# A conformer block on one core: order of the first projections, block sums of the up projection on VectorE, and a third plain pair

## The chip, the cores and the metric

The kernel runs on one core of a Trainium2 chip. The metric is the device time of one execution in microseconds; the time before is the median of three executions, 1815.06 us (1814.44 to 1816.28).

## What is computed

One layer of a hybrid block over 1024 tokens of width 1024, all in float32, cut here to what matters:

```python
h = rms_norm(x, norm1_g)
z = h @ w_in                                   # GLU value and gate, q, k, v, gate logits
a = a_val * sigmoid(a_gate)                    # the GLU: the "first projections"
a = silu(rms_norm(causal_depthwise_conv(a)))   # 31 taps
y_a = a @ w_conv_out
y_b = mixed_dilated_attention(q, k, v) @ w_attn_out
x = x + (g_a * y_a + g_b * y_b) @ w_out
h = rms_norm(x, norm2_g)
u = causal_depthwise_conv(h @ w_up)            # 1024 -> 2 x 2816, 3 taps
x = x + (silu(u_gate) * u_val) @ w_down
```

## The kernel before, in words

**Numbers and engines.** Every large product is made of matmuls on rounded operands: `split()` (L76, L77) copies a float32 tile to a rounded high part on ACT and subtracts it on DVE to get the low part, and each product is then three matmuls (high x high, high x low, low x high). So every operand, weights and activations, costs an ACT and a DVE operation before PE can use it. `stage()` (L81) loads a 128x1024 piece of weights into one of four `raw` buffers, `wsplit()` (L84 on) splits it into one of four `whi` and `wlo` buffers, `wpiece()` does both. PSUM is two double banks (`big_ps`, pool psA) and four single banks (`bank_ps`, pool psB).

**Who sets the order.** The code is written stage by stage, but a scheduler places each engine's instructions and may put an instruction ahead of others that stand earlier in the code, as far as buffers and data allow. An engine then works its list strictly in that order. So the order of the program text and the order on the engines differ.

**First stage (L204 to L240).** Eight token tiles of `x` are loaded; each is normalised (L221 to L223: squares on ACT, a power on POOL, a scaled multiply on DVE that writes `xs`), transposed on PE into two psum banks of psB (`tp_<tile>_<half of the channels>`, L190), and split from there into `hT` (L76, L77). `hT00` and `hT10` are the high and the low part of the first 512 tokens, `hT01` and `hT11` those of the other 512. The GLU loop (L227 on) then multiplies: `gemm_ch` runs `gemm_half` (L108 to L110) for the first 512 tokens (24 matmuls) and for the second (24), into a double bank per channel piece: `glug_0` (gate), `gluv_0` (value), and so on.

**The up projection (L541 to L658).** Its input (`h2raw`, transposed by `tq_<tile>_<half>`, L515, and copied by ACT, L516) and the weights are taken as 2x2 blocks, and the product is made with seven block products instead of eight, per pair `f` of a value and a gate channel piece (22 pairs). The activations' side needs the blocks b11, b12, b21, b22 and the sums t1 = b12 - b11, t3 = b22 - b12, t2 = t3 + b11 and t4 = b21 - t2, each split into `blk_t1` and so on. `sums(q)` does them for one half `q` of the columns at a time: t1 on POOL (L599), t3 and t2 on DVE (L600, L602); t4 follows on POOL (L619). The weights' side needs sums too (`up_sums`: L571 to L576 on DVE; `s12`, `s3g` and, split later, `s4`). The code of a pair: `up_first(f)` loads `raw_uv<f>` and makes the first two products (24 matmuls each pair of halves together, X and Z, of `h2left` with `hi_uv<f>`, `lo_uv<f>`) into the two halves of a double bank `xz_<f>`; these need no sums and are the "plain" products; `up_rest(f)` adds the products with t2, t1, t3, b22 and t4 (into X and a bank `y_<f>`), copies out on ACT (L631, L636, L643) and DVE (L632, L638, L641), applies the three taps and the gate (L647 to L652), and stores `dff[f]` (L653). Ahead of `sums(cols[1])` the code has the plain products of pairs 0 and 1.

**The down projection (L662 on)** loads `dff` (L676) and `w_down` (L682) in groups of two, again as seven block products into `dx_0`, `dx_1` (double banks) and four `dy` banks (`mac`, L703). The first two groups' activations are loaded ahead into `early0` and `early1`; the next go through tiles `gr` and, like the residuals `res` (L711), through memory that the blocks of the up projection hold until its last matmul. All DMAs named here are issued from SP's queue, in order.

## Time and profile before

| | |
|---|---|
| median of three executions | 1815.06 us (1814.44 to 1816.28) |
| the profiled execution | 1811.43 us |
| its span, from first to last instruction | 1809.6 us, so 1.8 us lie around it |
| granted TensorE clock, mean | 0.991 |

One execution was recorded. The profiled one is 3.6 us shorter than the median, so a time that is worked out from its rows is a difference, to be put on the median. A row of a timeline gives start, duration, engine, line, operation, output and inputs by the program's names without numbers, how many in a row, and in brackets the idle time before it with what ended it. A row of the waits gives the total in us, how often, and the longest. A row of the windows gives each engine's busy us, then the granted clock, the share of the DMA engines and GB/s. Engines are PE (TensorE), PEld (its weight loads), DVE (VectorE), ACT (ScalarE), POOL (GpSimd) and SP (SyncE). Matmuls overlap: one of 128x512 lasts 0.39 us and the next starts 0.23 us after it.

### The profile page before, as it was taken

The numbers are of one execution on the slowest core, as the hardware profiler recorded it, in microseconds if no ns is written. First come the engines' busy times: TensorE is split into PE (matmuls) and PEld (weight loads), VectorE is DVE, ScalarE is ACT, GpSimd is POOL, SyncE is SP. The second block draws the span as 40 slices with busy tenths as digits, with TensorE's granted clock in tenths as the row PEclk, the third lists the DMA queues.
The fourth block names the chain that finished last, engine by engine and source line by source line (L and its number), as shares of the span: only waits on it lengthen the run. The fifth ranks groups of instructions, "written<-read, shape, count | busy, mean of one in ns | idle before, by whom it ended". The sixth has DMA issues, their size and how long they took to land.

```text
span 1809.6 us, 22474 instructions
## 1 busy us (share of the span) xinstructions
PE 1765.8 (98%) x8244; PEld 1461.9 (81%) x8244; DVE 1318.8 (73%) x1798; ACT 771.6 (43%) x1202; POOL 195.8 (11%) x197
## 2 busy tenths in 40 slices
PE   7999999999999999999999999989999999999999
PEld 5888888888887888887888878768888888878887
DVE  5999999999735655666654543787777777789863
ACT  4111132232245656666655332545444554543441
POOL 1000133133002122222210000210000000000000
PEclk9999999999999999999999999999999999999999
DMA  5111145345549456666527543313222222389851
GB/s 203 59 47 47 41 134 163 116 134 157 157 173 246 145 158 175 180 165 179 164 70 279 169 160 133 104 48 107 80 82 81 71 95 91 116 303 335 298 180 47
DMA packets 142063, 257.57 MB, mean 142 GB/s; under 512 B 11265, under 2 KB 60545, under 8 KB 141953
## 3 DMA queue, kind: packets, MB, share of 16 engines
q1 hardware_dynamic: 141808, 255.61, 43.8%
q8 instruction: 65, 1.06, 0.3%
q10 hardware_dynamic: 144, 0.52, 0.1%
q14 instruction: 46, 0.37, 0.1%
HBM read 190.03 MB, written 66.06 MB: 142 GB/s over the span
## 4 chain that ended last, share of the span: by engine, by line
PE 53%; DMA 4%; DVE 4%; issue 1%; ACT 1%; SPq 1%; POOLq 0%; POOL 0%; DVEq 0%; ACTq 0%
PE xz L550 5%; PE xz L551 5%; PE xz L552 5%; PE dx L703 5%; PE dy L703 5%; DMA gg<-dya 2%; PE pp L400 2%; PE y L550 2%; PE y L552 2%; PE y L551 2%; PE ya L108 2%; PE ya L109 2%; PE ya L110 2%; PE o L408 2%; PE wo L126 1%; PE wo L127 1%
## 5 line engine op out<-in xcount | busy, mean ns | idle before, releaser
L253 DVE SCALAR_TENSOR_TENSOR cacc<-apad,pk,cacc 128x1024 f32<-128x1024 f32 x240 | 297.7, 1274 | 0.7
L125 PE MATMUL qkv<-hi_qkv,hT 128*128 128x512 f32 x384 | 151.8, 396 | 0.0
L127 PE MATMUL qkv<-hi_qkv,hT 128*128 128x512 f32 x384 | 150.0, 391 | 0.0
L126 PE MATMUL qkv<-lo_qkv,hT 128*128 128x512 f32 x384 | 149.4, 390 | 0.0
L389 DVE CUSTOM_DVE_ANT_0 p<-s,m 128x128 f32<-128x128 f32 (+7 forms) x128 | 95.1, 750 | 62.7 <-PE pp L400 39.0
L77 DVE TENSOR_TENSOR pl<-pp,ph 128x512 fp32r<-128x512 f32 x192 | 103.1, 549 | 49.1 <-ACT ph L76 48.6
L393 POOL TENSOR_SCALAR p<-p,st 128x128 f32<-128x128 f32 (+7 forms) x128 | 94.9, 748 | 335.5 <-DVE st L392 211.9
L76 ACT ACTIVATE ph<-pp 128x512 fp32r<-128x512 f32 x192 | 91.3, 487 | 92.2 <-PE pp L400 89.3
L649 DVE SCALAR_TENSOR_TENSOR u<-u,pk 128x1023 f32<-128x1023 f32 (+1 forms) x88 | 112.3, 1279 | 18.9 <-ACT u L647 18.5
L101 POOL TENSOR_TENSOR rs<-ss,mhalf 128x8 f32<-128x8 f32 (+1 forms) x40 | 80.3, 2010 | 353.1 <-DVE ss L100 353.0
L391 ACT ACTIVATE p<-p,st 128x128 f32<-128x128 f32 (+7 forms) x128 | 99.0, 776 | 14.6 <-DVE st L389 12.9
L108 PE MATMUL gate<-hT,hi_gt 128*128 128x512 f32 x256 | 101.8, 398 | 0.0
L109 PE MATMUL gate<-hT,hi_gt 128*128 128x512 f32 x256 | 100.8, 394 | 0.0
L110 PE MATMUL gate<-hT,lo_gt 128*128 128x512 f32 x256 | 100.3, 393 | 0.0
L400 PE MATMUL pp<-ident,p 128*128 128x128 f32 x576 | 94.4, 277 | 0.0
L127 PEld LDWEIGHTS qkv<-hi_qkv,hT 128*128 128x128 f32 x384 | 72.0, 188 | 15.3
L126 PEld LDWEIGHTS qkv<-lo_qkv,hT 128*128 128x128 f32 x384 | 72.2, 188 | 14.5 <-DVE lo_qkv L77 0.3
L125 PEld LDWEIGHTS qkv<-hi_qkv,hT 128*128 128x128 f32 x384 | 72.2, 188 | 14.0
L400 PEld LDWEIGHTS pp<-ident,p 128*128 128x128 f32 x576 | 69.5, 142 | 10.0 <-issue 0.2
L384 PE MATMUL s<-kh,q 128*128 128x512 f32 (+1 forms) x192 | 69.7, 368 | 7.3 <-DVE st L389 4.8
L408 PE MATMUL o<-ph,v 128*128 128x512 f32 x192 | 73.1, 381 | 3.6 <-ACT ph L76 1.8
L409 PE MATMUL o<-pl,v 128*128 128x512 f32 x192 | 70.5, 369 | 1.6 <-DVE pl L77 1.5
(269 smaller groups left out, 4610.4 us busy)
## 6 DMA issues: line engine op xcount, KB each, us to landing
wr<-w_down SPq DMA_DIRECT2D x45, 512.0 KB, 5.7
gr<-dff SPq DMA_DIRECT2D x62, 256.0 KB, 5.2
raw_qkv<-w_qkv SPq DMA_DIRECT2D x24, 512.0 KB, 3.9
raw_uv<-w_up SPq DMA_DIRECT2D x22, 512.0 KB, 3.3
raw_ug<-w_up SPq DMA_DIRECT2D x22, 512.0 KB, 3.3
dff<-u SPq DMA_DIRECT2D x22, 512.0 KB, 2.6
dv<-v SPq DMA_DIRECT2D x16, 512.0 KB, 3.2
raw_gt<-w_ch SPq DMA_DIRECT2D x16, 512.0 KB, 4.8
```

The lines of the kernel that those rows point to most:

```text
L108: pe.matmul(o, hi[:, k, :], ah[:, k, :], start=(k == 0), stop=False)
L109: pe.matmul(o, hi[:, k, :], al[:, k, :], start=False, stop=False)
L110: pe.matmul(o, lo[:, k, :], ah[:, k, :], start=False, stop=(k == KT - 1))
L125: pe.matmul(ps, ah, hi[:, k % 2, :], start=(k == 0), stop=False)
L126: pe.matmul(ps, ah, lo[:, k % 2, :], start=False, stop=False)
L127: pe.matmul(ps, al, hi[:, k % 2, :], start=False, stop=(k == KT - 1))
L253: dve.scalar_tensor_tensor(out=acc, in0=a[:, j : j + T], scalar=w(j), in1=acc, op0=ALU.mult, op1=ALU.add)
L400: pe.transpose(pp[:, qb * P : (qb + 1) * P], pts[qb][:, kt * P : (kt + 1) * P], ident)
L550: pe.matmul(o, wh[:, k, :], bh[:, k, :], start=(start and k == 0), stop=False, skip_group_check=not start)
L551: pe.matmul(o, wh[:, k, :], bl[:, k, :], start=False, stop=False, skip_group_check=not start)
L552: pe.matmul(o, wl[:, k, :], bh[:, k, :], start=False, stop=(k == 3), skip_group_check=not start)
L703: pe.matmul(banks[n], a[:, c], b[:, d], start=(start and i == 0 and m == 0), stop=(stop and i == nf - 1 and m == 2), skip_group_check=True)
```

## The change

Three edits. First, the code of the first stage normalises four tiles, splits the two first weight pieces, makes the first-half products of `glug_0` and `gluv_0`, then the other four tiles and the second halves; the two pieces' loads stay where they were. Second, `sums(q)` runs wholly on DVE: t13 = b12 - b11 (t1), t2 = b22 - t13 directly, then t13 is used again for t3 = b22 - b12; t4 moves from POOL to DVE. Third, the plain products of pair 2 are written ahead of the splits of b22 and t4; they go to two single banks `xzx_2` and `xzz_2` instead of a double bank.

```diff
+        def first_pair(half):
+
+            for ps, w in zip(glu0, wfirst):
+                for _ in gemm_half(ps[:, half * 512 : half * 512 + 512], w, hT, half):
+                    pass
+
+        for tt in range(4):
+            normed(tt)
+        wfirst = [wpiece(w_ch[c], n, raw) for c, n, raw in wfirst]
+        glu0 = [big_ps("glug_0"), big_ps("gluv_0")]
+        first_pair(0)
+        for tt in range(4, 8):
+            normed(tt)
+        first_pair(1)
...
-        def up_first(f):
+        def up_first(f, apart=False):
...
-            xz = big_ps(f"xz_{f}")
-            product(xz[:, 0:512], four(vh)[:, 0:4], four(vl)[:, 0:4], *left[0], True)
-            product(xz[:, 512:1024], four(vh)[:, 4:8], four(vl)[:, 4:8], *left[1], True)
+            if apart:
+                xz = (bank_ps(f"xzx_{f}"), bank_ps(f"xzz_{f}"))
+            else:
+                xz = big_ps(f"xz_{f}")
+                xz = (xz[:, 0:512], xz[:, 512:1024])
+            product(xz[0], four(vh)[:, 0:4], four(vl)[:, 0:4], *left[0], True)
+            product(xz[1], four(vh)[:, 4:8], four(vl)[:, 4:8], *left[1], True)
...
-            pool.tensor_tensor(out=t1, in0=b12[:, :, q], in1=b11[:, :, q], op=ALU.subtract)
-            dve.tensor_tensor(out=t3, in0=b22[:, :, q], in1=b12[:, :, q], op=ALU.subtract)
-            keep("t3", t3, q)
-            dve.tensor_tensor(out=t3, in0=t3, in1=b11[:, :, q], op=ALU.add)
-            keep("t2", t3, q)
-            keep("t1", t1, q)
-            t2.append(t3)
+            less = lambda o, x, y: dve.tensor_tensor(out=o, in0=x, in1=y, op=ALU.subtract)
...
+            less(t13, b12[:, :, q], b11[:, :, q])
+            less(t, b22[:, :, q], t13)
+            keep("t2", t, q)
+            keep("t1", t13, q)
+            less(t13, b22[:, :, q], b12[:, :, q])
+            keep("t3", t13, q)
+            t2.append(t)
...
         ups = [up_first(1)]
         sums(cols[1])
+        ups.append(up_first(2, True))
...
-            pool.tensor_tensor(out=t2[i], in0=b21[:, :, q], in1=t2[i], op=ALU.subtract)
+            dve.tensor_tensor(out=t2[i], in0=b21[:, :, q], in1=t2[i], op=ALU.subtract)
```

What the scheduler makes of it is seen in the order of instructions on the engines. The places below are in program order; a line number after the change is the one of the changed file, so L107 to L109 are the projections' matmuls, L189 the transposes, L532 `tq`, L567 to L569 the block products, L618 and L642 the sums, L726 `mac`, L699 the loads of `gr`, L734 the residuals.

**First place: PE in the first stage,** around the transposes of the last token tiles. Before, the transposes of tiles 4 and 5 stand 18 rows further up, among the first-half matmuls, and those of tiles 6 and 7 here:

```order
L109 MATMUL gluv_0_414<-hT10_190,hi_v0_168 128x512
L110 MATMUL gluv_0_414<-hT00_189,lo_v0_169 128x512
L190 MATMUL tp_6_0_326<-ident_70,xs_6_319 128x128 x4
L190 MATMUL tp_6_1_333<-ident_70,xs_6_319 128x128 x4
L190 MATMUL tp_7_0_347<-ident_70,xs_7_340 128x128 x4
L190 MATMUL tp_7_1_354<-ident_70,xs_7_340 128x128 x4
L108 MATMUL gluv_0_414<-hT00_189,hi_v0_168 128x512
L109 MATMUL gluv_0_414<-hT10_190,hi_v0_168 128x512
L110 MATMUL gluv_0_414<-hT00_189,lo_v0_169 128x512
L108 MATMUL glug_0_363<-hT01_191,hi_g0_162 128x512
L108 MATMUL gluv_0_414<-hT01_191,hi_v0_168 128x512
```

After, at the same rows:

```order
L108 MATMUL gluv_0_278<-hT10_182,hi_v0_273 128x512
L109 MATMUL gluv_0_278<-hT00_181,lo_v0_274 128x512
L189 MATMUL tp_4_0_334<-ident_70,xs_4_327 128x128 x4
L189 MATMUL tp_4_1_341<-ident_70,xs_4_327 128x128 x4
L189 MATMUL tp_5_0_355<-ident_70,xs_5_348 128x128 x4
L189 MATMUL tp_5_1_362<-ident_70,xs_5_348 128x128 x4
L189 MATMUL tp_6_0_376<-ident_70,xs_6_369 128x128 x4
L189 MATMUL tp_6_1_383<-ident_70,xs_6_369 128x128 x4
L189 MATMUL tp_7_0_397<-ident_70,xs_7_390 128x128 x4
L189 MATMUL tp_7_1_404<-ident_70,xs_7_390 128x128 x4
L107 MATMUL glug_0_277<-hT01_183,hi_g0_269 128x512
L107 MATMUL gluv_0_278<-hT01_183,hi_v0_273 128x512
```

All 48 first-half matmuls now stand ahead of the transposes of tiles 4 to 7, which follow one another; then comes the second half. The lists of ACT and DVE for this stage hold the same operations in the same order as before.

**Second place: PE and DVE where the up projection starts.** PE before, from the second-to-last transposes on; the other 21 matmuls of `xz_1` follow, and then twelve of `y_0` with `blk_t1`:

```order
L515 MATMUL tq_6_1_10120<-ident_70,x2_1_6_9987 128x128 x4
L550 MATMUL xz_1_10183<-h2left0_9424,hi_uv1_10179 128x512
L551 MATMUL xz_1_10183<-h2left0_9424,hi_uv1_10179 128x512
L515 MATMUL tq_7_0_10159<-ident_70,x2_1_7_10035 128x128 x4
L515 MATMUL tq_7_1_10165<-ident_70,x2_1_7_10035 128x128 x4
L552 MATMUL xz_1_10183<-h2left0_9424,lo_uv1_10180 128x512
L550 MATMUL xz_1_10183<-h2left0_9424,hi_uv1_10179 128x512
```

PE after; here `xz_1` is complete before `tq_7`, and four matmuls of the third pair stand ahead of `y_0`:

```order
L568 MATMUL xz_1_10183<-h2left1_9425,hi_uv1_10179 128x512
L569 MATMUL xz_1_10183<-h2left1_9425,lo_uv1_10180 128x512
L532 MATMUL tq_7_0_10159<-ident_70,x2_1_7_10035 128x128 x4
L532 MATMUL tq_7_1_10165<-ident_70,x2_1_7_10035 128x128 x4
L567 MATMUL xzx_2_10225<-h2left0_9424,hi_uv2_10221 128x512
L568 MATMUL xzx_2_10225<-h2left0_9424,hi_uv2_10221 128x512
L567 MATMUL xzz_2_10226<-h2left1_9425,hi_uv2_10221 128x512
L568 MATMUL xzz_2_10226<-h2left1_9425,hi_uv2_10221 128x512
L567 MATMUL y_0_10263<-blk_t1_10146,hi_s12_0_10131 128x512
L568 MATMUL y_0_10263<-blk_t1_10146,hi_s12_0_10131 128x512
L569 MATMUL y_0_10263<-blk_t1_10146,lo_s12_0_10132 128x512
```

The other 20 matmuls of the third pair follow behind the twelve of `y_0` with `blk_t1`, and then `y_0` with `blk_b22`. DVE before, from the first t3 difference on (POOL's t1 difference runs beside it):

```order
L600 TENSOR_TENSOR cb_t3_0_10149<-h2raw1_9423 128x1024
L538 TENSOR_TENSOR s1_7_10066<-ss2_9426 128x1
L100 TENSOR_SCALAR s1_7_10066<-s1_7_10066 128x1
L77 TENSOR_TENSOR blk_t1_10146<-cb_t1_0_10148,blk_t1_10146 128x4x256
L540 SCALAR_TENSOR_TENSOR x2_1_7_10035<-x2_1_7_10035,s1_7_10066,gb2_8796 128x1024
L77 TENSOR_TENSOR lo_uv1_10180<-raw_uv1_10177,hi_uv1_10179 128x1024
L77 TENSOR_TENSOR blk_t3_10147<-cb_t3_0_10149,blk_t3_10147 128x4x256
L77 TENSOR_TENSOR lo_s4_0_10274<-raw_uv0_10083,hi_s4_0_10273 128x512
L600 TENSOR_TENSOR cb_t3_256_10209<-h2raw1_9423 128x1024
L602 TENSOR_TENSOR cb_t3_0_10149<-cb_t3_0_10149,h2raw0_9422 128x1024
L77 TENSOR_TENSOR blk_b22_10175<-h2raw1_9423,blk_b22_10175 128x4x256 x2
L571 TENSOR_TENSOR s12_1_10314<-raw_ug1_10312 128x512
```

DVE after, from the first block sum on (`cb_t13` serves t1 and then t3):

```order
L618 TENSOR_TENSOR cb_t13_0_10148<-h2raw1_9423,h2raw0_9422 128x1024
L555 TENSOR_TENSOR s1_7_10066<-ss2_9426 128x1
L618 TENSOR_TENSOR cb_t2_0_10149<-h2raw1_9423,cb_t13_0_10148 128x1024
L99 TENSOR_SCALAR s1_7_10066<-s1_7_10066 128x1
L77 TENSOR_TENSOR lo_uv1_10180<-raw_uv1_10177,hi_uv1_10179 128x1024
L77 TENSOR_TENSOR blk_t1_10146<-cb_t13_0_10148,blk_t1_10146 128x4x256
L557 SCALAR_TENSOR_TENSOR x2_1_7_10035<-x2_1_7_10035,s1_7_10066,gb2_8796 128x1024
L77 TENSOR_TENSOR blk_t2_10145<-cb_t2_0_10149,blk_t2_10145 128x4x256
L618 TENSOR_TENSOR cb_t13_0_10148<-h2raw1_9423 128x1024
L642 TENSOR_TENSOR cb_t2_0_10149<-h2raw0_9422,cb_t2_0_10149 128x1024
L77 TENSOR_TENSOR blk_t3_10147<-cb_t13_0_10148,blk_t3_10147 128x4x256
L618 TENSOR_TENSOR cb_t13_256_10208<-h2raw1_9423,h2raw0_9422 128x1024
```

The subtraction of `blk_t3` for the first columns moves ahead of `blk_b22`; t4 of the first columns (L642) now stands here too; the second columns' `blk_t1` comes five rows behind the last one shown. On SP the load `raw_uv2` now comes ahead of `raw_ug1`, and its buffer is the one that `cb_t13_0` holds until `blk_t3` of the first columns is split.

**Third place: PE and SP at the end of the up projection.** PE before, the last matmuls of pair 21 and the first of the down projection; 47 more matmuls of `dx_0` and `dx_1` with `early0` and `early1` follow without a product of the up projection among them:

```order
L552 MATMUL xz_21_12867<-blk_t4_10176,lo_s3g_21_12903 128x512
L550 MATMUL xz_21_12867<-blk_t4_10176,hi_s3g_21_12902 128x512
L551 MATMUL xz_21_12867<-blk_t4_10176,hi_s3g_21_12902 128x512
L552 MATMUL xz_21_12867<-blk_t4_10176,lo_s3g_21_12903 128x512
L703 MATMUL dx_0_12997<-hi_a11_0_13009,early0_12992 128x512
L703 MATMUL dx_0_12997<-lo_a11_0_13010,early0_12992 128x512
```

PE after, where the last product of pair 21 (with `blk_t4`) begins:

```order
L726 MATMUL dx_0_12998<-hi_a11_2_13052,early1_12994 128x512 x2
L726 MATMUL dx_0_12998<-lo_a11_2_13053,early1_12994 128x512
L726 MATMUL dx_0_12998<-hi_a11_2_13052,early1_12994 128x512
L567 MATMUL xz_21_12868<-blk_t4_10176,hi_s3g_21_12903 128x512
L568 MATMUL xz_21_12868<-blk_t4_10176,hi_s3g_21_12903 128x512
```

And where that product of twelve matmuls ends:

```order
L567 MATMUL xz_21_12868<-blk_t4_10176,hi_s3g_21_12903 128x512
L568 MATMUL xz_21_12868<-blk_t4_10176,hi_s3g_21_12903 128x512
L569 MATMUL xz_21_12868<-blk_t4_10176,lo_s3g_21_12904 128x512
L726 MATMUL dx_1_12999<-hi_a11_0_13010,early0_12993 128x512
L726 MATMUL dx_1_12999<-lo_a11_0_13011,early0_12993 128x512
```

The 24 matmuls of `dx_0` with the early groups now stand ahead of that product, and the 24 of `dx_1` behind it. SP before:

```order
L682 DMA wr00_0_13224<-w_down 128x2x512
L711 DMA res_0_0_0_13041<-dx2_0_132 128x512
L711 DMA res_0_1_0_13043<-dx2_1_133 128x512
L711 DMA res_0_2_0_13045<-dx2_2_134 128x512
L711 DMA res_0_3_0_13047<-dx2_3_135 128x512
L676 DMA gr00_4_13079<-dff4_114 128x512
L676 DMA gr00_4_13079<-dff5_115 128x512
```

SP after:

```order
L705 DMA wr00_0_13225<-w_down 128x2x512
L676 DMA dff20_130<-u_20_12779 128x1024
L734 DMA res_0_0_0_13042<-dx2_0_132 128x512
L734 DMA res_0_1_0_13044<-dx2_1_133 128x512
L734 DMA res_0_2_0_13046<-dx2_2_134 128x512
L734 DMA res_0_3_0_13048<-dx2_3_135 128x512
L699 DMA gr00_4_13080<-dff4_114 128x512
L699 DMA gr00_4_13080<-dff5_115 128x512
```

The store of `dff20` now stands ahead of the residual loads; before it stood behind the `gr` loads.

25 lines of the change are left out of this document (13 added, 12 removed).

## Prediction

> **What bounds the kernel now.** The page comes first: which engine is full, and where it is not.
>
> ```profile
> span 1809.6 us, 22474 instructions
> ...
> PE 1765.8 (98%) x8244; PEld 1461.9 (81%) x8244; DVE 1318.8 (73%) x1798; ACT 771.6 (43%) x1202; POOL 195.8 (11%) x197
> ```
>
> TensorE is busy for 98% of the span. So the change is worth only what it takes from, or adds to, the 2% in which PE waits or runs at a lower clock. The waits of PE, read for the two stages that the change names (the first 60 us, then 1160 to 1210) and for the stage behind them, from 1610 on, are few:
>
> ```profile
> PE tp L190 <- DVE ss L100: 10.7, 2, 9.4
> PE glug L108 <- ACT hT L76: 0.5, 1, 0.5
> ...
> PE y L551 <- DVE blk_t L77: 4.7, 1, 4.7
> PE y L550 <- ACT hi_s L76: 2.7, 1, 2.7
> PE tq L515 <- issue: 0.8, 1, 0.8
> PE xz L550 <- ACT hi_uv L76: 0.8, 1, 0.8
> ...
> PE dx L703 <- ACT gh_t L76: 1.3, 1, 1.3
> ```
>
> Between 1210 and 1610 no wait is listed at all. The same in windows (busy time of PE, PEld, DVE, ACT and POOL, then the granted clock):
>
> ```profile
> 1160.00:1170.00 10.00, 8.39 (x44) 6.51 (x43) 9.62 (x10) 6.27 (x12) 3.03 (x3) 1.00 0.39 131
> 1170.00:1180.00 10.00, 5.30 (x24) 4.05 (x22) 10.00 (x9) 6.02 (x7) 3.00 (x1) 0.88 0.01 2
> 1180.00:1190.00 10.00, 9.73 (x33) 7.48 (x34) 10.00 (x10) 4.84 (x5) 3.30 (x1) 0.78 0.21 66
> 1190.00:1200.00 10.00, 7.33 (x33) 5.61 (x32) 8.47 (x9) 3.15 (x5) 3.30 (x1) 1.00 0.16 55
> ...
> 1210.00:1260.00 50.00, 49.89 (x218) 40.29 (x217) 41.09 (x45) 24.28 (x30) 0.00 (x0) 1.00 0.22 76
> ```
>
> In the 40 us where the up projection starts, PE is idle for 9.2 us (40 less 8.39, 5.30, 9.73 and 7.33) while DVE is full. Behind 1210 PE is full, DVE has 9 us of 50 free, and there is nothing to win. The lower clock of 1170 to 1190 is seen in the matmuls:
>
> ```profile
> 1174.79 0.39 PE L550 MATMUL y<-blk_t,hi_s 128*128 128x512 f32 x1
> 1179.88 0.80 PE L551 MATMUL y<-blk_t,hi_s 128*128 128x512 f32 x1 [4.70 <-DVE blk_t L77]
> ...
> 1180.90 0.63 PE L550 MATMUL y<-blk_t,hi_s 128*128 128x512 f32 x1
> ...
> 1184.31 0.42 PE L552 MATMUL y<-blk_t,lo_s 128*128 128x512 f32 x1
> ...
> 1196.15 0.50 PE L550 MATMUL y<-blk_b,hi_s 128*128 128x512 f32 x1 [2.67 <-ACT hi_s L76]
> ```
>
> After the idle 4.70 us eight matmuls take 3.41 us (1180.90 to 1184.31), 0.426 each; later the pitch is 0.227 (48 of them from 1594.47 to 1605.35, quoted below). So ten slow matmuls cost another 2.2 us, and everything that this stage can give is 9.2 + 2.2 = 11.4 us. After the 2.67 us wait, no such stretch follows.
>
> **The first stage.** The scheduler of the kernel before already starts the projections on half of the tokens, as the timelines of PE, ACT and DVE show:
>
> ```profile
> 20.18 0.80 PE L108 MATMUL glug<-hT,hi_g 128*128 128x512 f32 x1 [0.48 <-ACT hT L76]
> ...
> 27.60 1.91 PE L190 MATMUL tp<-ident,xs 128*128 128x128 f32 x16
> ...
> 34.15 1.91 PE L190 MATMUL tp<-ident,xs 128*128 128x128 f32 x16
> ...
> 37.35 0.50 PE L109 MATMUL glug<-hT,hi_g 128*128 128x512 f32 x1
> ...
> 34.78 2.07 ACT L76 ACTIVATE hT<-tp 128x512 fp32r<-128x512 f32 x4 [4.48 <-PE tp L190]
> ...
> 35.41 2.48 DVE L77 TENSOR_TENSOR hT<-tp,hT 128x512 fp32r<-128x512 f32 x4 [3.33 <-ACT hT L76]
> ```
>
> The order of ACT and DVE here does not change; PE's does. Before, the transposes of tiles 4 and 5 (27.60) lie among the first half's matmuls, and their splitting on ACT and DVE is hidden by those. After, all 48 first-half matmuls run first: 45 of them and 16 transposes (27.60 to 29.27, when the matmuls resume: 1.67) were done at 34.15, so without those transposes 48 are done at 34.15 - 1.67 + 3 x 0.227 = 33.2. Then come 32 transposes into four psum banks, so tile 6 waits for DVE to empty the banks of tile 4. DVE's first subtraction starts 1.26 us after the transposes begin (34.15 to 35.41), at 34.4, and one takes 0.60 ((2.48 - 0.68)/3). The second half's first matmul with the rounded remainder of hT (37.35 before) needs seven of them: 34.4 + 7 x 0.605 = 38.7. **+1.4 us**, and PE is full behind it, so all of it stays. Bounds: 0, if the order made nothing late, and +2.2, if all eight are needed and a bank's turn adds 0.2.
>
> **The start of the up projection.** The four 128x1024 operations of POOL go (L599, L619), and DVE gets four more. The rows give one of POOL's, then DVE's scaled multiply beside it and alone, and two whole splittings that follow on each other:
>
> ```profile
> 1160.19 2.43 POOL L599 TENSOR_TENSOR cb_t<-h2raw,h2raw 128x1024 f32<-128x1024 f32 x1 [0.55 <-ACT h2raw L516]
> ...
> 1160.29 3.41 DVE L540 SCALAR_TENSOR_TENSOR x<-x,s,gb 128x1024 f32<-128x1024 f32 x1
> ...
> 1167.18 1.28 DVE L540 SCALAR_TENSOR_TENSOR x<-x,s,gb 128x1024 f32<-128x1024 f32 x1
> 1168.38 1.22 DVE L77 TENSOR_TENSOR lo_uv<-raw_uv,hi_uv 128x1024 fp32r<-128x1024 f32 x1
> 1169.51 1.22 DVE L77 TENSOR_TENSOR blk_t<-cb_t,blk_t 128x1024 fp32r<-128x1024 f32 x1
> ```
>
> One operation beside each POOL operation is stretched by about 2.1 us (3.41 against 1.28). Ahead of blk_t1, for which PE waits at 1179.88, lie two such stretches, 4.3 us. In their place stand five more whole operations (three differences and two splittings, 1.13 us each by the pitch 1168.38 to 1169.51, 5.7 in all) and two half ones fewer (1.2): DVE wins nothing by then.
>
> Step by step: PE begins uv0 at 1159.7, and runs 48 uv matmuls (10.9) and two pairs of tq (0.8 each) without the waits of 0.8 us, since ACT rounds uv1 ahead of the block sums: free at 1172.1. Next in its order stand four matmuls of the third pair, which wait for hi_uv2, and **behind them queue y_0's twelve and all else on PE**. The load of uv2 is issued when DVE has split t3 of the first columns and so emptied a raw buffer: fifteen DVE operations from 1158.0 on (ten whole ones of 1.13, two scaled of 1.19, 0.8 in short ones, none stretched) end at 1172.7. Then 3.3 us for the load (the page's part on DMA, KB and us) and 1.06 for ACT (the tile's own view, least, median and most ns), behind blk_t1's rounding:
>
> ```profile
> raw_uv<-w_up SPq DMA_DIRECT2D x22, 512.0 KB, 3.3
> ...
> L76 ACT ACTIVATE hi_uv<-raw_uv x22: 1040/1062/1063, 1155.0 to 1564.5; 128x1024 fp32r<-128x1024 f32 x22
> ```
>
> hi_uv2 is there at 1177.8: PE idles 5.7 us, longer than before. blk_t1 follows after six more DVE operations, at 1179.7, as before (1179.88). So the wait for blk_t1 does not go. What is won: four uv2 matmuls lie inside the wait (0.9 us); the slow stretch starts 2.0 us earlier, so about 4.8 slow matmuls less, at 0.2 (1.0); the other 20 uv2 matmuls (4.5 us) stand between y_0's halves and cover the 2.67 us for hi_s4, and a small gap of 0.3. Sum 4.9; less 0.3 for short waits in the next pairs, which arrive earlier on a DVE that has not caught up: **-4.6 us**. Ends: 0, if the new wait eats what the cover gives, and -11.4, all of the above.
>
> The Trainium skill ("TensorE: Matmul & The Clock Gate", "What's actually happening") speaks against this step: an idle window of some 3.4 us halves the clock, and it takes about as much busy time to win it back, on a window that runs freely. The rows agree: 4.70 us cooled it, 2.67 did not, and it took 4.4 us. By that rule four short matmuls need not begin the warming, which would leave the slow stretch ending at 1184.3: the sum would be -3.6 and not -4.6.
>
> **From up to down.** The third pair shifts which psum buffer a pair gets, and with that PE's order at the end of the loop. Before, PE ends xz_21, then 48 dx matmuls on the early-loaded groups follow. Those cover a chain that starts at the last xz_21 matmul, whose memory the residuals take: four residual loads, two gr loads behind them on SP, ACT, DVE. Rows of the timelines of PE, SP and ACT, and of the chain that ended last:
>
> ```profile
> 1594.24 0.39 PE L552 MATMUL xz<-blk_t,lo_s3g 128*128 128x512 f32 x1
> 1594.47 0.39 PE L703 MATMUL dx<-hi_a,early 128*128 128x512 f32 x1
> ...
> 1605.35 0.39 PE L703 MATMUL dx<-hi_a,gh_b 128*128 128x512 f32 x1
> ...
> 1594.71 1.76 SPq L711 DMA_DIRECT2D res<-dx  x4
> ...
> 1596.99 5.75 DMA gr<-dff
> ...
> 1595.41 0.58 ACT L643 ACTIVATE u<-xz 128x512 f32<-128x512 f32 x1
> ...
> 1602.83 1.06 ACT L76 ACTIVATE gh_b<-gr 128x1024 fp32r<-128x1024 f32 x1 [3.54 <-DMA gr<-dff]
> ...
> 1603.92 1.22 DVE gl_b L77
> ```
>
> From 1594.63 the chain takes 9.3 us to gh_b and 10.5 to gl_b; the cover is 48 x 0.227 = 10.9. After, 24 of the 48 stand ahead of the last xz_21 product, and only 24 (5.45) behind it. The first of these waits for ACT's copy of xz_21, as they share a buffer (1.4 us in the rows: 1594.63 to 1595.99). PE idles 1.4, then until 9.3: 9.3 - 1.4 - 5.45 = 2.4, and 0.3 for gl_b behind four matmuls. With the sum's slack, 4.3; the later 1.3 us wait for gh_t goes, since ACT and DVE gain that time: **+3.0 us**. Ends: +1 (ACT's copy at once and later waits shorter too) and +7, below.
>
> **Nothing:** PE's order changes a little in the attention too; 0, within 0.5 either way, the size of the smaller gaps above. In the loop the pairs keep their work, PE has no wait and DVE a fifth free: 0.
>
> **Sum:** +1.4 - 4.6 + 3.0 = -0.2 us, made against the profiled execution, 1811.43 us (1809.6 span and 1.8 around it). That lies 3.6 under the median 1815.06 of three; the difference is carried over: **1814.9 us**.
>
> **Rivals.**
> *The wait for the blocks goes* (0.20). If DVE, without locks, has t1 two or three us earlier and uv2 with it, the gap stays near the 2.67 that did not cool the clock, and the stage gives -9: 1.4 - 9 + 3 = -4.6, 1810.5. For it: DVE is full there, and each us on it counts on PE. Against: the count of operations above.
> *Slower: the loads behind the last pairs* (0.18). In the new order of SP the store of u_20 stands ahead of the residual loads. u_20 is due about 1.8 us before the last xz_21 matmul; from the point where it is later, each us is one on PE. 2 us late, PE idles 4.9 us in a piece, and as after the 4.70 ten slow matmuls follow (2.0): 3.0 + 2.0 + 2.0 = +7. With 1.4 - 4.6 that is +3.8: 1818.9.
> *The change does what it says at the start*, and gains there: no room. The one wait behind 20.18 is 0.5 us; it is in the forecast, whose chance is 0.62.
>
> A measurement of this kernel tells 0.2%, 3.6 us, from no change. The forecast's own range is 1811.6 to 1818.2; with the rivals' bulk 1809.5 to 1818.9. Faster 0.20, same 0.62, slower 0.18.
>
> **What would show it.** In the profile after: transposes in one block at 33, and the second half resuming near 38.7 and not 37.4; no 128x1024 operation on POOL near 1165 to 1200, and no DVE operation above 1.3 us there; a wait of PE for hi_uv of 5 to 6 us at 1173, with a granted clock under 1 behind it; no wait for hi_s near 1195; three waits of dx near the transition, together 4 to 5 us. The prediction is wrong if the wait for hi_uv is under 3 us, if new waits appear in the loop, or if the store of u_20 holds the residuals.

## The result, and the profile after

The changed kernel takes **1816.21 us** (median of 22 runs, 1814.0 to 1821.82), the kernel before, run beside it, 1813.93 (22 runs, 1808.81 to 1818.61). The ratio is 1.0014 [1.0007, 1.0021]: slower by 2.5 us (1.3 to 3.8). The forecast was -0.2 us and 1814.9 us. The time lies within the range put on it (1811.6 to 1818.2), 1.3 us over the forecast, which stood on a median of three executions, 1815.06, that is 1813.93 over 22. The change itself went the other way. The loop, which was put at nothing, and the way from the up to the down projection cost more than the forecast had them.

The page of the changed kernel, span and engines:

```profile
span 1815.4 us, 22460 instructions
...
PE 1772.2 (98%) x8244; PEld 1463.7 (81%) x8244; DVE 1318.6 (73%) x1802; ACT 770.3 (42%) x1202; POOL 183.5 (10%) x193
```

The four operations have left POOL (197 to 193) and come to DVE (1798 to 1802), and DVE's busy time is the same to 0.2 us: its stretched operations are gone, whole ones stand in their place. The profiled execution took 1817.22 us, 5.8 more than the one of before. Of that, 3.5 is the choice of executions: the recorded one of before lay 2.5 us under the median of its 22 runs, the one of after 1.0 over. So two profiles are compared here stage by stage, at equal work: the time at which PE begins the same matmul.

**First stage.** Timeline of PE after; the last two rows are the second half's first matmul with the rounded part of `hT` and the first with the remainder:

```profile
33.64 4.46 PE L189 MATMUL tp<-ident,xs 128*128 128x128 f32 x32
38.19 0.50 PE L107 MATMUL glug<-hT,hi_g 128*128 128x512 f32 x1
...
39.24 0.50 PE L108 MATMUL glug<-hT,hi_g 128*128 128x512 f32 x1 [0.32 <-DVE hT L77]
```

The 32 transposes are one block from 33.64, and the last of these matmuls, which stood at 37.35 before, is at 39.24, right behind DVE's seventh subtraction: 1.9 us later.

**Start of the up projection.** The only wait of PE that is listed between 1155 and 1220, and windows over the same stage (busy time of PE, PEld, DVE, ACT and POOL, then the granted clock):

```profile
PE xzx L567 <- ACT hi_uv L76: 5.5, 1, 5.5
```

```profile
1170.00:1180.00 10.00, 6.53 (x34) 5.29 (x32) 9.70 (x9) 5.82 (x9) 0.11 (x1) 0.94 0.15 54
1180.00:1190.00 10.00, 8.01 (x28) 6.41 (x29) 10.00 (x10) 5.41 (x9) 0.00 (x0) 0.71 0.16 52
1190.00:1200.00 10.00, 10.00 (x46) 8.29 (x45) 9.09 (x13) 5.15 (x8) 0.00 (x0) 1.00 0.19 57
```

The waits for `blk_t1` (4.7) and `hi_s` (2.7) and the two of 0.8 are gone, and one for `hi_uv` of the third pair has come. PE is idle 5.5 us in these 30 us, and full from 1190 on, where before 2.7 us were idle.

**Loop.** In 300 us of it PE counts as full in both kernels; before first, then after:

```profile
1260.00:1560.00 300.00, 300.00 (x1325) 248.41 (x1324) 229.58 (x253) 145.31 (x174) 0.00 (x0) 1.00 0.24 83
```

```profile
1260.00:1560.00 300.00, 300.00 (x1320) 246.93 (x1319) 231.72 (x253) 144.13 (x174) 0.00 (x0) 1.00 0.23 82
```

"Full" hides a difference: five matmuls fewer were started in the same time, at the same clock. Busy time counts from a matmul's start to its end, and the 0.39 us of one cover the start of the next with 0.16 us to spare; a delay shorter than that shows in the distance of the starts. The loads of the weights (PEld), which have rows of their own, show it too. In the same 300 us PEld has one kind of wait after, and none before:

```profile
PEld y L569 <- DVE lo_s L77: 2.0, 7, 0.3
```

**From up to down.** Waits of PE between 1590 and 1640 after, and a window, after first and then before:

```profile
PE dx L726 <- ACT gh_b L76: 2.3, 1, 2.3
PE dx L726 <- ACT u L666: 1.4, 1, 1.4
```

```profile
1600.00:1620.00 20.00, 16.20 (x62) 12.27 (x61) 13.81 (x13) 9.97 (x11) 0.00 (x0) 0.91 0.94 341
```

```profile
1600.00:1620.00 20.00, 20.00 (x90) 16.57 (x89) 15.80 (x15) 8.02 (x9) 0.00 (x0) 1.00 1.05 401
```

Two waits, together 3.7 us, where before had only the 1.3 for `gh_t` at 1628, and behind them a clock of 0.91.

### The profile page after: what moved, and what is told of

It reads as the page before. It is cut to its first block, busy times and chain, and to the rows that moved or that the text cites. A ratio compares the mean times of both kernels' runs of the same rounds, so it can differ in the third digit from the quotient of the medians.

```text
span 1815.4 us, 22460 instructions
## 1 busy us (share of the span) xinstructions
PE 1772.2 (98%) x8244; PEld 1463.7 (81%) x8244; DVE 1318.6 (73%) x1802; ACT 770.3 (42%) x1202; POOL 183.5 (10%) x193
## 4 chain that ended last, share of the span: by engine, by line
PE 53%; DMA 6%; DVE 3%; ACT 1%; SPq 1%; issue 1%; DVEq 0%; ACTq 0%
PE dx L726 5%; PE xz L569 5%; PE xz L567 5%; PE xz L568 5%; PE dy L726 5%; DMA gg<-dya 2%; PE y L569 2%; PE y L567 2%; PE pp L417 2%; PE y L568 2%; PE ya L107 2%; PE wo L125 2%; PE ya L108 2%; PE wo L126 2%; PE wo L124 2%; PE ya L109 2%
## 5 line engine op out<-in xcount | busy, mean ns | idle before, releaser
L107 PE MATMUL gate<-hT,hi_gt 128*128 128x512 f32 x256 | 102.7, 401 | 0.0
L109 PE MATMUL gate<-hT,lo_gt 128*128 128x512 f32 x256 | 100.9, 396 | 0.0
```

The lines of the kernel that those rows point to most:

```text
L107: pe.matmul(o, hi[:, k, :], ah[:, k, :], start=(k == 0), stop=False)
L109: pe.matmul(o, lo[:, k, :], ah[:, k, :], start=False, stop=(k == KT - 1))
```

## The experiments

Each was run beside the kernel before on the same chip. The table gives each ratio as us (1813.5 times the ratio less 1) with its interval, and beside it, from the one profiled execution of each, how much later than in the profile of before PE begins the same matmul: at 37.35 us of before (first stage), and what is added from there between 1165.9 and 1263.8 (start), to 1591.3 (loop) and to 1664 (transition). In the long stretch between 37.35 and 1165.9 the kernels have the same work, and lie -2.0 to +3.8 us from before (e5, explained below, +7.3). This differs between executions of the same order too: e4 has PE's order of before there, and loses 3.6 us between 1066 and 1076, half of it to a longer wait for rounded weights (2.9 and not 1.1), half to slow matmuls behind it (clock 0.83 between 1070 and 1080, that of before 1.00).

| kernel | measured, us | first stage | start | loop | transition |
|---|---|---|---|---|---|
| after | +2.5 [1.3, 3.8] | +1.9 | -4.5 | +1.7 | +4.7 |
| e11, after once more | +1.8 [0.0, 3.6] | +1.2 | -4.1 | +1.9 | +3.7 |
| e1, first edit alone | +1.1 [-1.1, 3.4] | +1.3 | 0.0 | 0.0 | 0.0 |
| e2, sums on DVE alone | -4.0 [-6.0, -1.8] | -0.2 | -2.3 | 0.0 | 0.0 |
| e3, third pair alone | -3.1 [-5.4, -0.7] | +1.3 | +0.2 | 0.0 | 0.0 |
| e4, sums and third pair | -4.0 [-6.0, -2.0] | +0.1 | -2.5 | 0.0 | 0.0 |
| e5, after, value piece first | +3.4 [1.6, 5.4] | +1.7 | -1.5 | 0.0 | 0.0 |
| e6, after, six tiles ahead | -1.1 [-2.9, 0.7] | +0.7 | -2.5 | 0.0 | 0.0 |
| e7, after, residuals behind `gr` | -4.0 [-5.8, -2.4] | +2.3 | -4.7 | +1.6 | 0.0 |
| e8, e4 with the pair sooner | -4.5 [-6.5, -2.4] | +0.6 | -2.5 | 0.0 | 0.0 |
| e10, before, residuals behind `gr` | -2.0 [-4.0, -0.2] | +0.4 | 0.0 | 0.0 | -2.0 |
| e12, e8 with residuals behind `gr` | -5.4 [-7.6, -3.3] | +0.8 | +0.1 | 0.0 | -2.0 |

The first column of stages scatters by some 0.7 us whatever the kernel, since a stretch of matmuls 0.43 us apart from 21.9 us on ends at another time in each execution (23.6 us in before, 26.5 in e3). The start column scatters too: e8 and e12 have the same order on PE from the first matmul to 1591.3, yet differ by 2.6 us there, most of it by the granted clock. Windows of e8 first, then of e12:

```profile
1180.00:1190.00 10.00, 6.67 (x21) 5.06 (x22) 10.00 (x12) 4.12 (x6) 0.00 (x0) 0.83 0.00 0
1190.00:1200.00 10.00, 10.00 (x46) 8.28 (x45) 9.01 (x12) 6.25 (x8) 0.00 (x0) 1.00 0.32 105
```

```profile
1180.00:1190.00 10.00, 7.15 (x19) 5.25 (x20) 10.00 (x12) 4.49 (x6) 0.00 (x0) 0.62 0.00 0
1190.00:1200.00 10.00, 10.00 (x40) 8.12 (x40) 6.86 (x10) 4.05 (x6) 0.00 (x0) 0.87 0.31 105
```

The loop and the transition repeat far better: the seven profiles with the order of before in both, but for some rows at the loop's beginning (e1 to e6 and e8), lie within 0.02 us of it.

### e1_start: the first edit alone

```diff
+        for tt in range(4):
+            normed(tt)
...
+        first_pair(0)
+        for tt in range(4, 8):
+            normed(tt)
+        first_pair(1)
```

> Only the first edit (order of the first projections), sums and pairs as before. Theory A (each stage's time follows from the order that PE gets in that stage): the transposes of tiles 4 to 7 stand in one block, the second half of the projections starts about 1.6 us later, all else is as before: +1.6 us, from +1.2 to +2.0. Rival B (the 1.6 us seen in the profile after was partly the clock of that one execution): +0.5 to +1.0.

Measured: 1815.41 against 1813.33 us, 1.0006 [0.9994, 1.0019]. PE's timeline has the block of transposes, and the second half's first remainder matmul at 38.67:

```profile
33.07 4.46 PE L189 MATMUL tp<-ident,xs 128*128 128x128 f32 x32
...
38.67 0.50 PE L108 MATMUL glug<-hT,hi_g 128*128 128x512 f32 x1 [0.31 <-DVE hT L77]
```

The edit alone costs 1.3 us in the profile and 1.1 in the runs, where 0 is not excluded and the two theories can't be told apart. It does not make the loss by itself: loop and transition are those of before.

### e2_sums: the block sums on DVE alone

```diff
-            pool.tensor_tensor(out=t1, in0=b12[:, :, q], in1=b11[:, :, q], op=ALU.subtract)
...
+            less(t13, b12[:, :, q], b11[:, :, q])
+            less(t, b22[:, :, q], t13)
```

> Only the block sums and t4 on VectorE, no third pair, first stage as before. Theory A: PE still waits for blk_t1, some 8 us in all around 1173 to 1181, but the later wait for hi_s4 of 2.7 us and the slower VectorE operations beside POOL are gone: -2.3 us, from -1 to -4, with loop and transition to the down projection as before. Rival B (the gain needs the third pair as cover): 0 within 1 us.

Measured: 1810.51 against 1813.33, 0.9978 [0.9967, 0.999]. The waits at the start of the up projection:

```profile
PE y L550 <- ACT blk_t L76: 4.5, 1, 4.5
PE y L551 <- DVE blk_t L77: 2.9, 1, 2.9
PE y L552 <- DVE lo_s L77: 1.1, 1, 1.1
```

PE still waits for the blocks, in two pieces now, as the prediction's count of DVE's operations had it; the 2.67 for `hi_s` is gone with them.

### e3_pair: the third pair alone, sums on POOL as before

```diff
+            if apart:
+                xz = (bank_ps(f"xzx_{f}"), bank_ps(f"xzz_{f}"))
...
+        ups.append(up_first(2, True))
```

> Only the third plain pair ahead, in two single banks; sums on POOL as before. Theory A (order decides): PE's order in the loop and at its end is that of before, so no drift in the loop and no new wait at the transition; the third pair holds back VectorE's low part of s12 of pair 1, a wait of 3 to 4 us near 1191: +1.4 us, from 0 to +3. Rival B (the single banks of the third pair shift the psum buffers of all later pairs, as the prediction had it): about +2 us over the loop and +3 to +5 at the transition, +6 us or more.

Measured: 1810.99 against 1813.33, 0.9983 [0.997, 0.9996]. The profile has a start as long as that of before (+0.2): the 24 matmuls fill time, but waits of 2.2 for `hi_uv`, 1.8 for the copy of a pair and 1.1 for `lo_s` come in. The runs say 3.1 us faster, which neither theory had. Its recorded execution was 3.3 us over its median and that of before 2.5 under; which stretch the median gains in, one profile cannot tell. Some 1.6 us of its start are slow matmuls, 0.43 us apart and not 0.227, behind the wait of 1.8:

```profile
1233.32 0.50 PE L550 MATMUL xz<-blk_t,hi_s 128*128 128x512 f32 x1 [1.80 <-DVE u L637]
...
1235.63 0.63 PE L552 MATMUL xz<-blk_t,lo_s 128*128 128x512 f32 x1
1236.05 0.63 PE L550 MATMUL xz<-blk_t,hi_s 128*128 128x512 f32 x1
```

PE's order in the loop and at its end is that of before, though the third pair has its two single banks.

### e4_sums_pair: both of these, without the first edit

The diff is that of e2 and e3 together.

> Sums on VectorE and the third pair, without the first edit. Theory A (order decides): PE's order in the loop and at its end is that of before, so the 0.23 us per two pairs and the waits of dx at the transition are gone, and the gain at the start of the up projection stays, -4 us less 1 to 2 for short waits in pairs 2 and 3: -2.5 us, from -4 to -1. Rival B (third pair causes the loss in the loop and at the transition through its psum banks): -4 + 2 + 5 = +3 us.

Measured: 1810.7 against 1813.33, 0.9978 [0.9967, 0.9989]. The wait for `hi_uv` is that of after; then PE waits once more, for the copy that frees a bank in the next pair:

```profile
PE xzx L550 <- ACT hi_uv L76: 5.5, 1, 5.5
PE xzx L550 <- ACT u L637: 1.5, 1, 1.5
```

At 1226 us it had won 5.3, and gave 2.75 back in pairs 2 and 3, so that 2.5 stay. Loop and transition are those of before. Edits two and three are therefore worth some 4 us *without* the first, and the whole change loses 2.5: the parts don't add. Nor do these two between themselves: alone they measure -4.0 and -3.1, together -4.0. The order on PE says why: of the kernels here only those with all three edits as written (after, e7, e11 and the variant e9) have the new order in the loop and at its end.

### e5_swap: the value piece ahead of the gate piece

```diff
-            for ps, w in zip(glu0, wfirst):
+            for ps, w in list(zip(glu0, wfirst))[::-1]:
```

> The changed kernel with one word of the first edit turned round: the value's half products are written ahead of the gate's. All three edits are in, the transposes still stand in one block, and the scheduler gives PE the loop and the transition of before. Theory A (the loss is PE's order in the loop and at its end, which all three edits together happened to bring): the same +1.3 us at the start, the same 4 us won where the up projection starts less 2.5 given back in pairs 2 and 3, nothing lost in the loop and at the transition: -1 us against before, from -2.5 to +0.5, some 3.5 under the changed kernel. Rival B (the third pair's single banks, or the later start, cost the loop and the transition by themselves): +2.5 us, as the changed kernel.

Measured: 1816.94 against 1813.47, 1.0019 [1.0009, 1.003]. By its total it speaks for a loss in the first stage. The profile says otherwise: the gate's product ends last now, the next product in that double bank waits for the sigmoid, and slow matmuls follow.

```profile
PE glug L107 <- ACT sg L250: 3.3, 1, 3.3
```

That is a fault of this edit: at 48 us it is 3.1 us late, by 54 another 2.8. Its loop and transition have the order and the times of before (7.5 us late throughout both). A total alone would have misled here.

### e6_six: six tiles ahead of the first half

```diff
-        for tt in range(4):
+        for tt in range(6):
...
-        for tt in range(4, 8):
+        for tt in range(6, 8):
```

> The changed kernel with six token tiles normalised ahead of the first half products instead of four, so that the transposes of tiles 4 and 5 lie among these again and only those of 6 and 7 follow them; loop and transition are ordered as before. Theory A (the block of transposes is what the first edit costs): second half of the projections +0.3 to +0.7 us instead of +1.3, in sum -2 us against before, from -3.5 to 0. Rival B (the first stage differs by the clock of one execution, not by the order): no difference from the run with the two projections turned round, -1 us.

Measured: 1812.79 against 1813.47, 0.9994 [0.9984, 1.0004]. The transposes stand in two groups again, as before:

```profile
27.58 1.91 PE L189 MATMUL tp<-ident,xs 128*128 128x128 f32 x16
...
34.79 1.91 PE L189 MATMUL tp<-ident,xs 128*128 128x128 f32 x16
...
38.00 0.50 PE L108 MATMUL glug<-hT,hi_g 128*128 128x512 f32 x1 [0.21 <-DVE hT L77]
```

With them loop and transition went back to the order and the times of before: one number in the first stage moves instructions 1500 us later.

### e7_residuals: the changed kernel with the residual loads behind `gr`

```diff
-            if fs is groups[1]:
-                rs11 = [residual(0, n, 0) for n in range(4)]
...
+            if fs is groups[-1]:
+                rs11 = [residual(0, n, 0) for n in range(4)]
```

> The changed kernel with the four residual loads moved behind the loads of gr; PE's order in the loop and at its end stays that of the changed kernel. Theory A (at the transition PE waits for the chain last xz_21 matmul, residual loads, gr loads, ACT, VectorE): the drift of 2.2 us over the loop stays; the wait for gh_b falls from 2.3 to about 0.5, the slow stretch behind it goes, and the transition costs 2 instead of 5 us: 3.5 us under the changed kernel, from 2 to 5 under, about -1 us against before. Rival B (the loads land no sooner, since weights and the store of u_20 share their queues): under 1 us of difference from the changed kernel, +1.5 to +2.5 against before.

Measured: 1810.56 against 1813.47, 0.9978 [0.9968, 0.9987]. SP's DMAs where the memory of the blocks comes free, after first and then e7 (start, time over which so many were issued):

```profile
1601.24 1.76 SPq L734 DMA_DIRECT2D res<-dx  x4
...
1603.05 4.81 SPq L699 DMA_DIRECT2D gr<-dff  x7
```

```profile
1601.97 3.19 SPq L699 DMA_DIRECT2D gr<-dff  x7
1605.21 3.74 SPq L734 DMA_DIRECT2D res<-dx  x4
```

`gr` is issued 1.8 us sooner behind the last product, and the wait for `gh_b` is gone; only the 1.4 for ACT's copy is left. PE is busy in 18.60 of the 20 us where after had 16.20, and the clock stays whole:

```profile
1600.00:1620.00 20.00, 18.60 (x82) 15.09 (x81) 13.98 (x13) 9.86 (x11) 0.00 (x0) 1.00 0.90 325
```

The transition adds 0.0 in place of 4.7, and the runs differ from those of after by 6.5. The loop's 1.6 stays, so it is another loss. The 6.5 is more than the 3.7 to 4.7 of the two transitions, and than the 2 to 5 expected; the rest is open (below).

### e8_pair_sooner: e4 with the third pair ahead of the second columns' sums

```diff
-        ups = [up_first(1)]
+        ups = [up_first(1), up_first(2, True)]
         sums(cols[1])
-        ups.append(up_first(2, True))
```

> Sums on VectorE and the third pair, without the first edit, and the plain products of pair 2 written ahead of the sums of the second columns: all 24 then stand ahead of y_0 on PE. Theory A (PE's wait there is for whatever comes last on VectorE, so it moves behind the pair): the wait for hi_uv of 5.5 us stays, 20 matmuls (4.5 us) then fill part of the time to blk_t1, and a wait of about 3.5 us for blk_t1 follows; no gain over the run with sums and pair, -0.8 us to 0 against it, about -3.5 us against before. Rival B (pair 2 sooner removes the long idle piece and with it the slow clock): 3 us or more under the run with sums and pair.

Measured: 1808.67 against 1813.47, 0.9975 [0.9964, 0.9987]; beside e4 (0.9978) no difference can be told. The 5.5 us for `hi_uv`, which was expected to stay, goes, and 3.3 for `blk_t` with 1.6 for a copy and 1.4 without a releaser take its place:

```profile
PE y L551 <- DVE blk_t L77: 3.3, 1, 3.3
PE xzx L550 <- ACT u L636: 1.6, 1, 1.6
```

### e9_own: the changed kernel with a buffer of its own for `s4`

```diff
-            s4h, s4l = [four(t) for t in wsplit(s4, f"s4_{f}")]
+            if f < 3:
+                s4h, s4l = [four(t) for t in wsplit(s4, f"s4_{f}")]
+            else:
+                s4t = p4r.tile([P, 1024], F32R, tag="st", bufs=2, name=f"s4t_{f}")
+                split(s4t[:, 0:512], s4t[:, 512:1024], s4)
```

> The changed kernel in which s4 of the pairs from 3 on is split into a tile of its own (the two buffers that the t2 sums leave free), not into the shared buffers for high and low parts; PE's order in the loop stays that of the changed kernel but for one matmul, the end of the loop is ordered worse, so only the loop is read. Theory A (the drift comes from hi_s4 waiting for the buffer that the last t4 product, four matmuls ahead, still reads): the pitches of 0.25 and 0.33 us at y with blk_b22 in every second pair go, and what drift is left stands elsewhere, under 0.2 us per two pairs. Rival B (VectorE's load in this order is the cause): the same 0.23 us per two pairs at y with blk_b22.

One execution: 1821.42 us against 1813.01 (median of before on this chip). It was made for the loop. There, in every second pair of after, four matmuls of the `h2left` product stand between the last reader of a `whi` buffer (`xz` with `blk_t4`) and the `y` product with the `s4` that ACT rounds into that same buffer. PE, ACT and DVE of after at one such place:

```profile
1410.80 0.39 PE L568 MATMUL xz<-blk_t,hi_s3g 128*128 128x512 f32 x1
...
1412.39 0.39 PE L568 MATMUL y<-blk_b,hi_s 128*128 128x512 f32 x1
1412.64 0.50 PE L569 MATMUL y<-blk_b,lo_s 128*128 128x512 f32 x1
1412.98 0.39 PE L567 MATMUL y<-blk_b,hi_s 128*128 128x512 f32 x1
```

```profile
1411.23 0.63 ACT L76 ACTIVATE hi_s<-raw_uv 128x512 fp32r<-128x512 f32 x1 [1.31 <-PE xz L568]
```

```profile
1411.90 0.69 DVE L77 TENSOR_TENSOR lo_s<-raw_uv,hi_s 128x512 fp32r<-128x512 f32 x1 [0.72 <-ACT hi_s L76]
```

```profile
1412.64 0.19 PEld L569 LDWEIGHTS y<-blk_b,lo_s 128*128 128x128 f32 x1 [0.29 <-DVE lo_s L77]
```

The last reader of the buffer ends at 1411.19; ACT, which had waited for it, rounds until 1411.86, and DVE subtracts until 1412.59. The loads of weights here begin with the matmul ahead (the one for the matmul at 1412.39 comes at 1412.17): this load was due at 1412.39, and comes at 1412.64, 0.05 behind DVE. Its matmul starts with it, only 0.02 later than due, but lasts 0.50 and not 0.39, and the next starts 0.34 behind it and not 0.227. In the kernel before, 24 matmuls with `h2left` lie between (at such a place from 1406.79 to 1412.01), and the distance of starts stays 0.227 through its whole loop. In after eight distances at this product exceed that by 0.11 each; two at 1581.40 and 1581.84, in pair 21, exceed it by 0.21 and 0.11, and smaller ones, most of them at the same product, add up with them to the 1.7 us of the table.

In e9 the distances at this product are regular again, but longer ones appear at the next, as here 0.44 and 0.33 us where `xz` with `blk_t3` begins:

```profile
1422.05 0.39 PE L569 MATMUL y<-blk_t,lo_s 128*128 128x512 f32 x1
1422.49 0.50 PE L567 MATMUL xz<-blk_t,hi_s3g 128*128 128x512 f32 x1
1422.82 0.40 PE L568 MATMUL xz<-blk_t,hi_s3g 128*128 128x512 f32 x1
```

There the load of the weights waits for ACT's copy out of `xz` (L657), 0.5 us at most. So the delay at the buffer's place goes with the buffer, but that didn't win the time back. How much the next dependence costs in the order of after, e9 can't say: besides the one matmul that was expected, four of `y` with `blk_t` stand elsewhere in every second pair. Its total is mostly the end of its loop, where it loses 8.4 us between 1500 and 1591.3 of before.

### e10_before_res: the kernel before with the residual loads behind `gr`

The diff is that of e7, on the kernel before.

> The kernel before with the four residual loads moved behind the gr loads, nothing else. Theory A (the chain of loads behind the last xz_21 matmul sets what is late after it): PE's wait of 1.3 us for gh_t2 near 1626 and the small one behind it go, -1.5 us, from -2.5 to -0.5. Rival B (that wait is for ACT's own work): 0 within 0.5 us.

Measured: 1810.85 against 1813.01, 0.9989 [0.9978, 0.9999]. The 1.3 us for `gh_t` goes, and the transition is 2.0 shorter. The same four loads cost 2.0 us in the old order, and 3.7 to 4.7 with what follows them in the new one.

### e11_again: the changed kernel once more

> The changed kernel once more, for a second profile. Theory A (its terms follow from the order): second half of the projections 1.3 to 2.3 us later than before, -4.5 us where the up projection starts, +1.7 us over the loop, +3 to +5 at the transition (the last by whether a slow stretch follows the waits): +2.5 us. Rival B (part of it was this one execution): the loop or the transition differs by over 1 us.

Measured: 1815.5 against 1813.01, 1.001 [1.0, 1.002]. The waits come again, and with them the loop's 1.9:

```profile
PE dx L726 <- ACT gh_b L76: 2.5, 1, 2.5
PE dx L726 <- ACT u L666: 1.4, 1, 1.4
```

What differs is what follows them: distances of starts over 0.227 us add 2.1 us behind the two waits in the first profile, 1.6 of it by slow matmuls, and 0.5 in this one, where the clock stays 1.00. In e9, which has waits of 1.41 and 2.35 there, the slow matmuls come as in the first.

### e12_best: e8 with the residual loads behind `gr`

The diff is that of e8 with that of e7; the first edit is left out.

> Sums on VectorE, pair 2 ahead of the sums of the second columns, residual loads behind the gr loads, no first edit. Theory A (terms add): -2.4 us at the up projection's start, -1.5 us from the residuals, 0 at the first stage, in the loop and at the transition: -4 us, from -6 to -2. Rival B (what the residuals free is eaten by the next wait in the down projection): as the run without them, -2.5 us.

Measured: 1807.52 against 1813.01, 0.997 [0.9958, 0.9982]: 5.4 us faster than before, where the changed kernel is 2.5 slower: the fastest of all that were run. Its profiled stages show the 2.0 of the transition; its start would show some 2.5 more if it went as in e8, whose order it has.

## Why the prediction was wrong, step by step

**First stage, +1.4: right.** The block of transposes makes DVE's seventh subtraction late. The kernels with the block (after, e1, e5, e7, e11) begin the remainder matmul 1.7 us late on average, those with the old order (e2, e3, e4, e8, e10, e12) 0.5, so the block costs 1.2.

**Start of the up projection, -4.6: right.** The wait for `hi_uv` was reckoned at 5.7 and is 5.5; it cools the clock, as the 4.70 did (0.71 in the window behind it); `hi_s` is covered. Three profiles of this order give -4.5, -4.1 and -4.7. In the pairs behind it 0.4 is given back, where 0.3 was reckoned; in the other order of the loop (e4) it is 2.75, so the new order is also what keeps this gain. By the Trainium skill ("TensorE: Matmul & The Clock Gate", "What's actually happening") the sum would have been -3.6; the three values lie nearer the sum without it. The slow distances last 3.5 to 4.8 us in these profiles (4.4 before), counted from the first of the four matmuls of the third pair (1181.99 to 1185.87 in after), which speaks for these four counting.

**In the loop the pairs keep their work, PE has no wait: 0. This step failed,** by +1.6 to +1.9 us. The pairs do keep their work, but not their order, and "PE waits for nothing" is no proof of no wait. The order of the changed kernel was there to be read: from the end of the last reader of a rotating buffer to the load of the remainder that is written there next there are 1.20 us of matmuls (1411.19 to 1412.39), against a chain of 1.40 us on ACT and DVE (1411.19 to 1412.59). The kernels with the old order of the loop, e5 and e6 with variants of all three edits among them, lose nothing there. The chain of each product should have been set against the matmuls that cover it in the loop too, as it was behind it.

**From up to down, +3.0: the mechanism was right, the size was not.** The two waits were reckoned at 1.4 and 2.4, and are 1.4 and 2.3 to 2.5; the 0.3 for `gl_b` is not listed for PE, but is there in the starts (0.46 us behind the matmul at 1611.49, and 0.34 behind the next); the 1.3 for `gh_t` went (1.4 + 2.4 + 0.3 is 4.1, so the 4.3 of the forecast has 0.2 from no row); the transition measured +3.7 and +4.7. The mis-sized term is what follows the waits: it was put at nothing, since a single idle piece of 2.67 had cooled nothing before, and the starts behind them lost 0.5 us in one execution, of which `gl_b` is 0.3, and 2.1 in another, of which 1.6 are slow matmuls (clock 0.74 from 1610 to 1615). Also each wait takes 0.16 more than its idle time, since the overlap of two matmuls is lost with it. The rows of the costly one, from the first wait on:

```profile
1602.62 0.50 PE L726 MATMUL dx<-hi_a,early 128*128 128x512 f32 x1 [1.41 <-ACT u L666]
...
1610.69 0.50 PE L726 MATMUL dx<-hi_a,gh_b 128*128 128x512 f32 x1 [2.33 <-ACT gh_b L76]
...
1612.63 0.63 PE L726 MATMUL dx<-lo_a,gh_b 128*128 128x512 f32 x1
...
1615.19 0.63 PE L726 MATMUL dx<-lo_a,gh_b 128*128 128x512 f32 x1
```

**"The third pair shifts which psum buffer a pair gets, and with that PE's order at the end of the loop": refuted** as the cause named. e3, e4, e6 and e8 have that pair in those banks, and the order of before. Of the kernels run, it changes only in those with all three edits as written; the first edit with only one of the others was not run. Why the scheduler turns there is open, and no run was made to find out.

**The sum.** By the means of the profiles 1.2 - 4.3 + 1.8 + 4.2 = +2.9, against +2.5 measured; the forecast was 1.4 - 4.6 + 0 + 3.0. The slower rival was not it either: its trigger, the store of u_20 late, didn't come:

```profile
1599.02 0.34 SPq L676 DMA_DIRECT2D dff<-u  x1
```

That is 2.2 us ahead of the residuals at 1601.24, which were released by the last product. But its price, slow matmuls behind the idle time, came without it. "The wait for the blocks goes" did not come out either: the stage gave -4.1 to -4.7, not -9.

**What stays open.** Most kernels measure better than the sum of their four stages: e2 and e4 by some 1.5 us, e8 by 2.6, e7 by 3.2, e12 by 4.3 and e3 by 4.6. The profile of before is a short execution of its kernel (2.5 under the median), but it is not short in the last three columns, where e1 and e10 repeat the stages that they share with it to 0.1 us; it is in the first stage (0.5 under the other kernels of that order) and in the long stretch behind it (some 1.6 under the others). Slow matmuls explain most of 2.6 in e12's start and 1.6 of e3's. The rest, of e3 and e7 above all, is open, and it is as large as the effect of the change. So the stages show where time goes; that they add up to +2.9 beside +2.5 measured is in part luck. That the residuals' place is worth 2.0 us to the kernel before is seen in two profiles (e10, e12) and in the runs of e10, whose interval ends near 1.

## What to carry to other kernels

Where a scheduler sets the order, an edit is priced by the whole new order and not by the stage it names: compare it from start to end, and in each loop count the matmuls between the last reader of a rotating buffer and the first use of its next content, against the chain that fills it. A listed wait of PE shows only what is longer than the overlap of two matmuls; for less, look at the waits of its weight loads (PEld), and compare the start of the same matmul in two traces. On a queue that issues in order, loads that are needed late belong behind those that are needed next, which here was worth 2.0 us in the old order and 3.7 to 4.7 in the new one.

## What the runs showed of the hardware

Two idle pieces of TensorE, 1.4 and 2.3 us with 5.7 us of work between them, were followed by a clock of 0.91 over 20 us and 1.6 us lost to slow matmuls, though one of 2.67 in the kernel before had no such effect; in another execution of the same order, behind 1.4 and 2.5, no matmul was slow. In e3 a single piece of 1.80, with no other listed in the 35 us ahead of it, was followed by eight slow matmuls (clock 0.83 in the window from 1230 to 1240), though pieces of 1.4 to 1.6 at the like place in e4, e5, e6, e8 and e12 were not. Nor does length alone decide: at 1067 to 1070 us of before, where PE waits twice for rounded weights, 1.12 and 1.70 (before) and 1.56 and 1.77 (e10) were followed by no slow matmul, and the shorter 0.89 and 1.82 of e11 by thirteen, 0.43 us apart. The Trainium skill's page ("TensorE: Matmul & The Clock Gate", "What's actually happening") gives a window of some 3.4 us idle; the 5.5 and the 4.70 agree with it, the 1.80 of e3 does not, and how shorter pieces count, these runs do not settle. In the loop of after a matmul whose weights came 0.25 us late started 0.02 late, and the next 0.11 more (0.34 behind it and not 0.227): this delay is listed for PEld and not for PE. The executions of one kernel lie up to 10 us apart (1808.81 to 1818.61 before), more than the effects, so medians and equal-work stages were needed for both.
